# Depthwise convolution on TensorE: six channel tiles as matmuls over 4 tap groups x 32 channels

## The chip, the cores and the metric

One core of a Trainium2 chip. The time is device microseconds (us) of one execution of the whole program. A core has five engines that work beside each other, each through its own queue in order: TensorE (PE; its weight loads are listed apart as PEld), VectorE (DVE), ScalarE (ACT), GpSimd (POOL) and SyncE (SP), which here issues nearly all transfers.

## What is computed

A trunk of four layers over 256 tokens of 1024 channels. Each layer adds a token mixer and then a squared-ReLU feed-forward of width 4096. The mixers are retention, Conformer convolution, stick-breaking attention, retention. The change touches the convolution, which occurs once:

```
h = xn @ pw1_w + pw1_b
a, gate = jnp.split(h, 2, axis=-1)
h = a * jax.nn.sigmoid(gate)
h = lax.conv_general_dilated(            # depthwise: each channel by itself,
    h, dw_w[:, None, :].astype(h.dtype), # 31 taps, causal
    window_strides=(1,), padding=[(CONV_WIDTH - 1, 0)],
    dimension_numbers=('NWC', 'WIO', 'NWC'), feature_group_count=D_MODEL) + dw_b
h = layer_norm(h, ln_w, ln_b)
h = jax.nn.silu(h).astype(xn.dtype)
return h @ pw2_w + pw2_b
```

All is float32.

## The kernel before

Activations lie with channels on partitions: eight channel tiles of 128 partitions x 256 tokens. Weights stream from memory once, in a fixed order, on SP's queue: `unit` (L324) loads a chunk of 1 MB into one of three buffers `raw`; a chunk holds two units of 128x1024, and each unit is split into a high part `wh` by ACT (L336) and a low part `wl` by DVE (L337), in a pool of five. A buffer `raw` is loaded again when DVE has split its second unit.

The convolution starts with the first pointwise projection, pair of tiles by pair (`pair_b`, matmuls L456 to L458 into PSUM tiles `acc`); for each pair DVE and ACT compute the gated unit (`gate_in` L874, L877; `glu` L882, L887) and leave the result behind 30 zero columns in a tile `hc`. So tap w of a tile is the slice of 256 columns from w on.

The 31 taps of the eight tiles are shared out by hand:
- tile 0 on DVE (`tap_dve`, L927: multiply and add into PSUM tiles `mis`), later tiles 6 and 7 (into `acc`) and part of tile 5;
- tile 1, then tile 4 and the rest of tile 5 on ACT and POOL (`tap_pool`: ACT multiplies, L934, POOL adds, L936);
- tiles 2 and 3 and six taps of tile 5 on PE (`tap_pe`, L939): a diagonal 128x128 stationary matrix, built by POOL (L864) long before, times the slice of 256 columns, in fp32; each such matmul is two records in the trace.

The layer norm needs sums over all channels. `shift_a` takes column sums of finished tile 1 (L373), `shift_b` copies them (DVE, L967) and broadcasts them by two matmuls (L380) and an ACT copy (L384); the result `Gb` is subtracted from every tile when it is finished: `fin` (L980, L981), `fin_pe` (L984, one DVE instruction that reads PSUM), `fin_5` (L990 to L993). `stats` squares the tile on ACT (L945) and adds column sums of values and squares, four matmuls with one moving column for each tile (L373). The sums go to DVE (`lnv`, L1042), then mean, rsqrt, two broadcasts (L380), `warm` (L281: matmuls on ones that nothing reads), normalisation (POOL L1053, DVE L1061, ACT L1062), the split into high and low parts (L348, L349) and the second projection `out_proj`.

The order inside the stage is a table: each step is given a place on an axis by the numbers in `TP`, the steps are sorted by it (`ev`, `at`), and PE, DVE, POOL and ACT each keep that program order (`manual_schedule`). Weight chunks are issued and split where the program's own order and the buffers let them.

Of the kernel before, what the change touches and what calls it, by code (L numbers as in the profile page):

```python
# [8 lines left out]
F32 = mybir.dt.float32  # L9
# [6 lines left out]
P = 128  # L16
# [13 lines left out]
DST = 6  # chunk with which the first decay table comes  # L30
# order of the steps in stick-breaking attention
# [6 lines left out]
# order of the steps in the convolution: each group's place on one axis  # L38
TP = dict(
    pe2=42, pe3=0.0, pe5=4.4, po1=5.8, po1s=0.5, dv0=15.2, dv0s=1.05, po4=40.0, dv6=52.4,  # L40
    po5=64.8, dv5=80.5, sum1=38.7, sha=43.5, shb=44.0, shc=52.5, st1=55.1, fi0=50.0, st0=56.4,
    fi2=64.2, st2=71, fi4=71.4, st4=75.6, fi6=77.81, fi3=80.43, st6=80.2, st3=86.12, fi5=84.2,
    st5=95.3,
)
# taps of channel tile 5 on PE and on DVE
PE5, DV5 = 6, 7
# [72 lines left out]
# ---------------------------------------------------------------- parameter columns  # L119
def _param_cols():  # L120
    off, cols = 0, {}

    def add(key, n):
        nonlocal off
        cols[key] = off
        off += n

    add("norm_mix", DEPTH * 8)
    add("norm_ffn", DEPTH * 8)
    add("final", 8)  # L130
# [6 lines left out]
    add("dww", 8 * CW)  # L137
# [14 lines left out]
def _pack_params(inp):  # L152
# [16 lines left out]
    for t in range(8):  # L169
        out[:, PCOL["dww"] + t * CW : PCOL["dww"] + (t + 1) * CW] = dw[:, t * P : (t + 1) * P].T  # L170
# [26 lines left out]
def _consts():  # L197
# [10 lines left out]
    put("o32", np.full((P, 32), 1 / DK))  # L208
    put("sel", (r[:, None] // 32 == np.arange(4)[None, :]) / 32)
# [21 lines left out]
class Trunk:  # L231
    def __init__(self, ctx, tc, xT, w, prm, cst, out):
# [11 lines left out]
        self.prp = pool("prp", 3)  # L244
        self.acc_p = pool("acc", 4, space=bass.MemoryType.PSUM)
# [8 lines left out]
        self.rawt = self.raw.tile([P, UPC * 1024], F32, name="raw0", tag="raw")  # L254
# [12 lines left out]
        self.raw1 = self.raw.tile([P, UPC * 1024], F32, name="raw1", tag="raw")  # L267
# [8 lines left out]
    # keeps the tensor engine's clock up where it has to wait  # L276
# [7 lines left out]
    # ---- small helpers  # L284
# [29 lines left out]
    def unit(self, key):  # L314
# [29 lines left out]
    # a k-tile to [hi | lo]  # L344
# [7 lines left out]
    # ---- rsqrt of a column tile by Newton steps  # L352
    def rsqrt(self, m, n, tag):
# [6 lines left out]
        # of third order, with a = -m y^2: y (15 + 10 a + 3 a^2) / 8 = 3/8 y ((a + 10/3) a + 5); 3/8 is left out here  # L360
# [4 lines left out]
        # Newton's step, with 3/8 taken in  # L365
# [5 lines left out]
    # column sums over partitions: dst[tok, 0] (+)= sum_p src[p, tok] * scale  # L371
# [3 lines left out]
    # [tok, 2 columns] -> [128, 256] on all partitions  # L375
# [14 lines left out]
    # ---- RMSNorm: z = x * w as hi/lo, squares summed for r  # L390
# [50 lines left out]
    # ---- weights stationary: one unit (4 k-tiles x 256 columns) into a bank [2 m-tiles x 256 tok]  # L441
# [18 lines left out]
    # the same into half a bank for each m-tile  # L460
# [13 lines left out]
    # into a bank for each m-tile: [wh zh + wl zh | wh zl]  # L474
# [43 lines left out]
    # ---- feed-forward  # L518
# [42 lines left out]
    # ---- final RMSNorm: x * w turned to rows, scaled per token on the way out  # L561
# [28 lines left out]
    # x * w to rows, two pairs to a bank for each token tile  # L590
# [9 lines left out]
    # the last pair, its second m-tile after its first  # L600
# [50 lines left out]
    # ---- retention  # L651
    def retention(self, j, nxt):
# [34 lines left out]
        # mean squares: each head on 32 rows beside the others, then per token [tok, (token tile, q or k, head)]  # L687
# [8 lines left out]
        # per-token factors  # L696
# [19 lines left out]
        for h in range(RH):  # L716
# [5 lines left out]
            for t in range(2):  # L722
# [8 lines left out]
                else:  # L731
                    # token tile 0, seen by all tokens, as hi and lo
# [100 lines left out]
    # ---- activations stationary: one unit (2 k-tiles x 512 columns) into two banks [tok, 512]  # L833
# [13 lines left out]
    # ---- Conformer convolution  # L847
    def conv(self, j, nxt):
# [4 lines left out]
        todo = [(2, w) for w in range(CW)] + [(3, w) for w in range(CW)] + [(5, w) for w in range(CW - PE5, CW)]  # L853
        dgs = {}

        # diagonal stationary operands, four taps to a tile
        for i in range(0, len(todo), 4):
            d = self.bigt()
            grp = todo[i : i + 4]
            while grp:  # L860
                t, w = grp[0]
                n = sum(1 for x in grp if x[0] == t)
                o = (4 - len(grp)) * P if len(todo[i : i + 4]) == 4 else (len(todo[i : i + 4]) - len(grp)) * P
                nc.gpsimd.tensor_mul(  # L864
                    v3(d[:, o : o + n * P], n, P), self.id.unsqueeze(1).to_broadcast([P, n, P]),
                    self.p("dww", t * CW + w, n).unsqueeze(2).to_broadcast([P, n, P]),
                )
                for e in range(n):
                    dgs[t, w + e] = d[:, o + e * P : o + (e + 1) * P]
                grp = grp[n:]  # L870
# [9 lines left out]
        def glu(p, pa, sg):  # L880
            va = self.tmp()
            nc.vector.tensor_mul(v3(va, 2, S), v3(pa, 2, S), self.b2(rb))  # L882
            for f in range(2):
                s = slice(f * S, (f + 1) * S)
                o = self.bigt()
                nc.gpsimd.memset(o[:, : CW - 1], 0.0)
                nc.vector.scalar_tensor_tensor(  # L887
                    out=o[:, CW - 1 : CW - 1 + S], in0=va[:, s], scalar=self.p("pw1b", 2 * p + f), in1=sg[:, s],
# [19 lines left out]
        tap = lambda t, w: hc[t][:, w : w + S]  # L908
        wc = lambda t, w: self.p("dww", t * CW + w)
# [4 lines left out]
        r0, r1, r4, r5 = halves(self.mis), halves(self.bigt), halves(self.bigt), halves(self.bigt)  # L914
        r6, r7, pb2, pb3 = self.acc()[:, :S], self.acc()[:, :S], self.acc(), self.acc()
        pb2, pb3, pb5 = pb2[:, :S], pb3[:, :S], pb2[:, S:]

        # running sums of taps; the first op of a sum starts it
# [350 lines left out]
```

## Time and profile before

| | |
|---|---|
| three runs | 1398.76, 1400.78, 1402.77 us; median 1400.78 |
| the profiled execution, its span | 1399.4 us (no other time of it is listed) |
| PE, DVE, ACT, POOL busy | 99%, 73%, 57%, 14% of the span |
| first pointwise projection of the convolution | 404 to 446 us |
| taps, shift and column sums | 446 to 492 us |
| norm, then the second projection from 499 us on | 492 to 524 us |

In the tables that follow, a row of a timeline gives start, duration, engine, source line, operation, names written and read, shapes, how many instructions follow each other, and in brackets the idle time just before with the instruction that ended it. Busy times of PE overlap, since matmuls are pipelined; the distance between starts tells what one costs.

### The profile page before, as it was taken

Reading aid. Unit: us, or ns where it says so; the run is one execution under the profiler, and the core shown is the slowest. Engines: PE = TensorE matmul, PEld = TensorE weight load, DVE = VectorE, ACT = ScalarE, POOL = GpSimd, SP = SyncE. Lnnn points to the kernel's source line nnn. Section 1 sums busy time; section 2 is a strip of 40 time slices with the busy share of each in tenths; the row PEclk is TensorE's granted clock in tenths of the full one; section 3 lists DMA queues with packets and bytes.
Section 4 is the critical chain, followed back from the end, with each engine's and each line's share of the span. In section 5 each row is a group of like instructions: output and inputs, shape, how many; then the busy total and the mean of one; then the engine's idle time right before and its main releaser. Section 6 shows DMA issues by size and latency. Waiting matters only on the chain.

```text
span 1399.4 us, 22116 instructions
## 1 busy us (share of the span) xinstructions
PE 1378.7 (99%) x8742; PEld 1239.7 (89%) x8742; DVE 1015.0 (73%) x1725; ACT 798.0 (57%) x1213; POOL 194.2 (14%) x189
## 2 busy tenths in 40 slices
PE   8999999999998999999999999999999999999998
PEld 6789999888998888888988898888987999988887
DVE  6976778775679978765578578765587687788643
ACT  6645456664457656655468666654565455555442
POOL 3201003000259920000000010000110010100011
PEclk9999999999999999999999999999999999999999
DMA  7554445555554025555543345555454444555550
GB/s 266 199 181 146 156 151 208 184 181 190 174 181 169 10 91 187 202 183 183 195 179 136 114 158 185 200 187 184 178 181 153 171 140 170 181 181 183 192 192 35
DMA packets 34808, 235.77 MB, mean 168 GB/s; under 512 B 3984, under 2 KB 4624, under 8 KB 7056
## 3 DMA queue, kind: packets, MB, share of 16 engines
q1 hardware_dynamic: 34416, 233.83, 47.1%
q8 instruction: 68, 1.11, 0.3%
q10 hardware_dynamic: 288, 0.52, 0.1%
q14 instruction: 36, 0.29, 0.1%
HBM read 233.29 MB, written 1.05 MB: 167 GB/s over the span
## 4 chain that ended last, share of the span: by engine, by line
PE 94%; DVE 3%; issue 1%; ACT 1%; DMA 1%; SPq 0%; DVEq 0%; ACTq 0%
PE acc L483 32%; PE acc L484 17%; PE acc L458 8%; PE acc L457 8%; PE acc L456 8%; PE acc L843 4%; PE acc L844 4%; PE acc L845 4%; PE acc L939 2%; PE mis L373 1%; DVE wl L337 1%; DVE mis L927 1%; PE mis L380 1%; PE acc L472 1%; PE acc L471 1%
## 5 line engine op out<-in xcount | busy, mean ns | idle before, releaser
L337 DVE TENSOR_TENSOR wl<-raw,wh 128x1024 fp32r<-128x1024 f32 (+1 forms) x442 | 555.1, 1257 | 290.5 <-ACT wh L336 285.5
L336 ACT CAST wh<-raw 128x1024 fp32r<-128x1024 f32 (+1 forms) x442 | 461.6, 1045 | 426.8 <-PE acc L483 213.9
L483 PE MATMUL acc<-z,wh 128*128 128x512 f32 x1248 | 438.1, 396 | 6.1 <-ACT wh L336 3.3
L484 PE MATMUL acc<-z,wl 128*128 128x256 f32 x1248 | 348.4, 282 | 0.2 <-DVE wl L337 0.2
L483 PEld LDWEIGHTS acc<-z,wh 128*128 128x128 f32 x1248 | 233.4, 188 | 62.3 <-ACT wh L336 4.4
L483 PE MATMUL acc<-big,wh 128*128 128x512 f32 x768 | 267.7, 393 | 0.0
L484 PEld LDWEIGHTS acc<-z,wl 128*128 128x128 f32 x1248 | 236.2, 189 | 3.0 <-DVE wl L337 1.5
L484 PE MATMUL acc<-big,wl 128*128 128x256 f32 x768 | 215.2, 280 | 0.0
L483 PEld LDWEIGHTS acc<-big,wh 128*128 128x128 f32 x768 | 143.8, 187 | 32.7
L457 PE MATMUL acc<-big,wh 128*128 128x256 f32 x576 | 162.3, 283 | 1.0 <-DVE big L349 1.0
L456 PE MATMUL acc<-big,wh 128*128 128x256 f32 x576 | 161.4, 284 | 1.1 <-DVE big L348 1.1
L458 PE MATMUL acc<-big,wl 128*128 128x256 f32 x576 | 162.3, 283 | 0.0
L484 PEld LDWEIGHTS acc<-big,wl 128*128 128x128 f32 x768 | 145.1, 189 | 0.0
L419 POOL TENSOR_TENSOR t<-t,t 128x512 f32<-128x512 f32 x25 | 39.1, 1563 | 733.7 <-DVE z L404 456.9
L456 PE MATMUL acc<-z,wh 128*128 128x256 f32 x416 | 118.3, 285 | 0.0
L458 PE MATMUL acc<-z,wl 128*128 128x256 f32 x416 | 118.1, 284 | 0.0
L457 PE MATMUL acc<-z,wh 128*128 128x256 f32 x416 | 117.8, 284 | 0.0
L457 PEld LDWEIGHTS acc<-big,wh 128*128 128x128 f32 x576 | 110.4, 192 | 1.2 <-DVE big L349 1.2
L456 PEld LDWEIGHTS acc<-big,wh 128*128 128x128 f32 x576 | 109.5, 192 | 2.1 <-DVE big L348 1.6
L458 PEld LDWEIGHTS acc<-big,wl 128*128 128x128 f32 x576 | 110.4, 192 | 0.0
L502 ACT COPY t<-acc 128x256 f32<-128x256 f32 x180 | 65.1, 371 | 58.2 <-PE acc L484 58.2
L843 PE MATMUL acc<-wh,z 128*128 128x512 f32 x224 | 87.8, 394 | 0.0
(240 smaller groups left out, 1943.6 us busy)
## 6 DMA issues: line engine op xcount, KB each, us to landing
raw<-in_w SPq DMA_DIRECT2D x216, 1024.0 KB, 4.8
raw<-in_w SPq DMA_DIRECT2D x6, 512.0 KB, 7.7
x<-in_x SPq DMA_DIRECT2D x4, 256.0 KB, 5.8
raw<-in_w SPq DMA_DIRECT2D x4, 256.0 KB, 7.4
cst<-in_cst SPq DMA_DIRECT2D x4, 192.0 KB, 5.0
cst<-in_cst SPq DMA_DIRECT2D x1, 532.0 KB, 8.8
out<-t SPq DMA_DIRECT2D x2, 256.0 KB, 2.7
out<-t ACTq DMA_DIRECT2D x2, 256.0 KB, 2.9
```

The costliest lines, as they stand in the source:

```text
L336: nc.scalar.copy(hi[:, s], src[:, s])
L337: nc.vector.tensor_sub(lo[:, s], src[:, s], hi[:, s])
L419: (nc.vector if p == 3 and self.quick else nc.gpsimd).tensor_add(a, self.sq, q)
L456: nc.tensor.matmul(o, wh[:, kk, cs], ah, start=st, stop=False, **kw)
L457: nc.tensor.matmul(o, wh[:, kk, cs], al, start=False, stop=False, **kw)
L458: nc.tensor.matmul(o, wl[:, kk, cs], ah, start=False, stop=en, **kw)
L483: nc.tensor.matmul(ps[m], wh[:, kk, cs], a, start=first and kk == 0, stop=False, **kw)
L484: nc.tensor.matmul(ps[m][:, :S], wl[:, kk, cs], a[:, :S], start=False, stop=last and kk == 3, **kw)
L502: nc.scalar.copy(o[:, s], ps[m][:, S:])
L843: nc.tensor.matmul(ps[t], zh[:, s], wh[:, kk], start=k == 0, stop=False, skip_group_check=True)
L844: nc.tensor.matmul(ps[t], zh[:, s], wl[:, kk], start=False, stop=False, skip_group_check=True)
L845: nc.tensor.matmul(ps[t], zl[:, s], wh[:, kk], start=False, stop=k == 7, skip_group_check=True)
```

## The change

Tiles 2 to 7 go to PE, tile 0 stays on DVE and tile 1 on ACT and POOL. A matmul no longer has 128 channels and one tap, but 32 channels and four taps:

- `spread(d)` writes two finished tiles `hc[d]`, `hc[d+1]` (128x287) to DRAM by two transfers and reads them back by four, each into 32 partitions: partition 32 s + c holds, for channel c of each group of 32, the row moved by 8 s columns, 263 wide. It goes into a buffer `raw`, which is 2104 columns wide instead of 2048. It is called for tiles 2, 4 and 6, on SP's queue.
- `taps_pe(d, g)`, for round g of 8: four matmuls, one for each group j of 32 channels, on the column group 32 j to 32 j + 31 of the array. The stationary operand is a strip of 128x32 with the weights of taps g - 1, g + 7, g + 15 and g + 23 (`strip`, built by POOL in 12 instructions of 128x512), the moving one 256 columns of the spread rows from column g on, the result 32 partitions of the tile's PSUM half.
- `stats(d)` is one matmul of a constant 128x32 with all 512 columns (values and squares), onto one of four column groups; ACT copies the result and four column-sum matmuls with one column finish it. The squares are steps of their own (`square`).
- Two channel tiles share one PSUM tile, `acc`.

```
+        def spread(d):
+            rows = self.dram.tile([2, 4, 32, HL], F32, name=self.nm("hd"), tag="hd")
+            for i in range(2):
+                nc.sync.dma_start(rows[i].rearrange("j c u -> (j c) u"), hc[d + i][:, :HL])
+            t = self.raw.tile([P, RAWW], F32, name=self.nm("raw"), tag="raw")
+            for s in range(4):
+                nc.sync.dma_start(
+                    v3(t[32 * s : 32 * s + 32], 8, HW),
+                    rows.rearrange("i j c u -> c (i j) u")[:, :, NG * s : NG * s + HW],
+                )
+            for i in range(2):
+                h4[d + i] = t[:, i * 4 * HW : (i + 1) * 4 * HW]
...
             pa = self.pair_b("conv_pw1_w", j, p * 256, self.zs)
+            if p == 3:
+                spread(2)
+                spread(4)
             glu(p, pa, gate_in(p, pg))
+        spread(6)
...
-        def tap_pe(t, w, o, first, last):
-            nc.tensor.matmul(o, dgs[t, w], tap(t, w), start=first, stop=last, **kw)
+        def taps_pe(d, g):
+            for j in range(4):
+                nc.tensor.matmul(
+                    pb[d][32 * j : 32 * j + 32], strip[d][g // 4][:, ((g % 4) * 4 + j) * 32 : ((g % 4) * 4 + j + 1) * 32],
+                    h4[d][:, j * HW + g : j * HW + g + S], start=g == 0, stop=g == NG - 1, **kw,
+                )
...
         def stats(d):
-            nc.scalar.activation(out=cc[d][:, S:], in_=cc[d][:, :S], func=AF.Square)
             n = L["n"]
             L["n"] += 1
-            for t in range(2):
-                for e in range(2):
-                    i = t * 2 + e
-                    self.colsum(
-                        L["st"][:, i : i + 1], cc[d][:, e * S + t * P : e * S + (t + 1) * P], self.sc(1024),
-                        n == 0 and i == 0, n == 7,
-                    )
+            o = 32 * (n % 4)
+            nc.tensor.matmul(L["st"][o : o + 32], self.c("o32", 32), cc[d], start=n < 4, stop=n > 3, **kw)
...
+        for i, d in enumerate(PET):
+            t0 = TP["pe"] + TP["pes"] * i
+            for g in range(NG):
+                at(t0 + 0.43 * g, taps_pe, d, g)
+            at(max(t0 + 3.9, TP["f2"]), fin_pe, d, pb[d])
+            at(max(t0 + 4.0, TP["f2"]), square, d)
...
+        sm, st = self.tmp(), self.mis()
+        nc.scalar.copy(sm, L["st"])
+        for t in range(2):
+            for e in range(2):
+                i = t * 2 + e
+                self.colsum(st[:, i : i + 1], sm[:, e * S + t * P : e * S + (t + 1) * P], self.sc(128))
```

Comments of the source are gone and lines have moved; the lines of the changed kernel that the order rows name are L338 and L351 (weight load and DVE's split), L883 and L886 (`spread`), L966 (`taps_pe`), L981 (`stats`), L1007 (`fin_pe`), L1043 (`lnv`).

Three places where the order of instructions matters. The first is PE at the last two channel tiles (`acc_4828` is the PSUM tile of tiles 6 and 7, `raw_4808` their spread rows, `big_4818` to `big_4821` the finished tiles 4 to 7, `mis_5026` the sums):

```order
L966 MATMUL acc_4828<-raw_4808,big_4232 32x256 x16
L981 MATMUL mis_5026<-big_4818,cst 32x512 [waits Activation_49]
L981 MATMUL mis_5026<-big_4819,cst 32x512 [waits Activation_49]
L966 MATMUL acc_4828<-raw_4808,big_4234 32x256 x4
L966 MATMUL acc_4828<-raw_4808,big_4234 32x256 [waits DVE_49]
L966 MATMUL acc_4828<-raw_4808,big_4234 32x256 x11
L966 MATMUL acc_4828<-raw_4808,big_4236 32x256 x16
L981 MATMUL mis_5026<-big_4820,cst 32x512 [waits Activation_49]
L981 MATMUL mis_5026<-big_4821,cst 32x512 [waits Activation_49]
```

Where PE ran single taps of tiles 3 and 5 in one row, it now runs the first round of tile 7 (four matmuls) and then waits for DVE, which has to read tile 6 out of the same PSUM tile. Tile 5 has the same wait for tile 4.

The second is DVE over the same time (`acc_4827` is the PSUM tile of tiles 4 and 5; `raw_5300`, `raw_5358` and `raw_5416` are the next three weight chunks):

```order
L1007 SCALAR_TENSOR_TENSOR big_4818<-acc_4827,prm,Gb_5024 128x256 [waits PE_49]
L351 TENSOR_TENSOR wl_5303<-raw_5300,wh_5302 128x1024 [waits DMAHW3_49,Activation_49]
L351 TENSOR_TENSOR wl_5331<-raw_5300,wh_5330 128x1024 [waits Activation_49]
L1007 SCALAR_TENSOR_TENSOR big_4819<-acc_4827,prm,Gb_5024 128x256 [waits PE_49]
L351 TENSOR_TENSOR wl_5361<-raw_5358,wh_5360 128x1024 [waits DMAHW4_49,Activation_49]
L351 TENSOR_TENSOR wl_5389<-raw_5358,wh_5388 128x1024 [waits Activation_49]
L1007 SCALAR_TENSOR_TENSOR big_4820<-acc_4828,prm,Gb_5024 128x256 [waits PE_49]
L351 TENSOR_TENSOR wl_5419<-raw_5416,wh_5418 128x1024 [waits DMAHW5_49,Activation_49]
L1007 SCALAR_TENSOR_TENSOR big_4821<-acc_4828,prm,Gb_5024 128x256 [waits PE_49]
L1043 COPY lnv_5188<-mis_5182 128x4 [waits PE_49]
```

Before, five splits of the second projection's weights stood among the last pointwise steps and the taps of tile 0; now four stand between the fin of tile 4 and that of tile 6.

The third is SP's queue from the spread of tiles 6 and 7 on:

```order
L883 DMA hd_4805<-big_4799 128x287 [waits DMAHW5_49,DVE_49,Pool_49]
L883 DMA hd_4805<-big_4802 128x287 [waits DMAHW6_49,DVE_49,Pool_49]
L886 DMA raw_4808<-hd_4805 32x8x263 [waits DMAHW6_49,DMAHW5_49,Activation_49]
L886 DMA raw_4808<-hd_4805 32x8x263
L886 DMA raw_4808<-hd_4805 32x8x263 [waits DMAHW1_49]
L886 DMA raw_4808<-hd_4805 32x8x263 [waits DMAHW2_49]
L338 DMA raw_5300<-in_w 128x2048 [waits DMAHW3_49,PE_49]
L338 DMA raw_5358<-in_w 128x2048 [waits DMAHW4_49,DMAHW3_49,DVE_49]
L338 DMA raw_5416<-in_w 128x2048 [waits PE_49]
L338 DMA raw_5496<-in_w 128x2048 [waits DMAHW4_49,DVE_49]
```

Before, the chunk in the first of these places followed the last chunk of the first projection at once and waited for DVE alone. Now `raw_5300` stands behind the three spreads and waits for PE, which reads the spread rows of tile 3 in that buffer; `raw_5358` goes into the buffer of `raw_5300` and waits for its landing and its split; `raw_5416` waits for the taps of tile 5.

## Rows read from the trace of the kernel before

**Rows 1.** The page: busy time of each engine, share of the span and instructions; and the chain of work that ended last, by line, as shares of the span.
```profile
PE 1378.7 (99%) x8742; PEld 1239.7 (89%) x8742; DVE 1015.0 (73%) x1725; ACT 798.0 (57%) x1213; POOL 194.2 (14%) x189
PE acc L483 32%; PE acc L484 17%; PE acc L458 8%; PE acc L457 8%; PE acc L456 8%; PE acc L843 4%; PE acc L844 4%; PE acc L845 4%; PE acc L939 2%; PE mis L373 1%; DVE wl L337 1%; DVE mis L927 1%; PE mis L380 1%; PE acc L472 1%; PE acc L471 1%
```

**Rows 2.** Windows by stage: the stretch, its length, busy time (and instructions) of PE, PEld, DVE, ACT and POOL, the granted clock of PE as a share of full speed, the share of DMA time, GB/s.
```profile
404.00:453.00 49.00, 44.96 (x365) 43.99 (x364) 44.98 (x69) 36.67 (x63) 33.26 (x33) 0.99 0.44 153
453.00:487.00 34.00, 33.74 (x160) 29.68 (x160) 32.36 (x78) 23.39 (x51) 32.80 (x48) 0.91 0.07 28
```

**Rows 3.** Timeline of PE from the last pointwise matmul to the norm.
```profile
445.80 0.28 PE L458 MATMUL acc<-z,wl 128*128 128x256 f32 x1
445.92 1.89 PE L939 MATMUL acc<-big,big 128*128 128x256 f32 x8
...
453.26 1.22 PE L380 MATMUL mis<-cst,lns 128*128 128x128 f32 x4 [2.96 <-DVE lns L967]
454.27 13.69 PE L939 MATMUL acc<-big,big 128*128 128x256 f32 x52
...
469.99 0.95 PE L373 MATMUL mis<-cst,big 128*128 128x1 f32 x8
470.80 12.34 PE L939 MATMUL acc<-big,big 128*128 128x256 f32 x56
```

**Rows 4.** Timeline of DVE, late pointwise steps and the first instruction of the norm.
```profile
441.18 1.77 DVE L887 SCALAR_TENSOR_TENSOR big<-t,prm,t 128x256 f32<-128x256 f32 x2
442.88 1.76 DVE L337 TENSOR_TENSOR wl<-raw,wh 128x1024 fp32r<-128x1024 f32 x1
...
449.59 0.67 DVE L882 TENSOR_TENSOR t<-acc,rb 128x512 f32<-128x512 f32 x1
450.19 1.21 DVE L337 TENSOR_TENSOR wl<-raw,wh 128x1024 fp32r<-128x1024 f32 x1
451.32 1.81 DVE L887 SCALAR_TENSOR_TENSOR big<-t,prm,t 128x256 f32<-128x256 f32 x2
...
492.13 0.16 DVE L1042 COPY lnv<-mis 128x4 f32<-128x4 f32 x1 [2.00 <-PE mis L373]
```

**Rows 5.** Groups of instructions by line, engine and shape, from 430 to 560 us (the last one from 300 to 400 us): count, busy time, mean ns of one, idle time before them.
```profile
L936 POOL TENSOR_TENSOR big<-big,pr 128x256 f32<-128x256 f32 x63 | 51.3, 854 | 2.6 <-ACT pr L934 2.6
L337 DVE TENSOR_TENSOR wl<-raw,wh 128x1024 fp32r<-128x1024 f32 x28 | 37.9, 1352 | 8.8 <-ACT wh L336 8.5
L336 ACT CAST wh<-raw 128x1024 fp32r<-128x1024 f32 x27 | 28.2, 1045 | 10.3 <-PE acc L457 6.3 <-PE acc L483 3.4 <-ACT t L414 0.5
L927 DVE SCALAR_TENSOR_TENSOR acc<-big,prm,acc 128x256 f32<-128x256 f32 x60 | 23.7, 476 | 0.0
L945 ACT ACTIVATE big<-big 128x256 f32<-128x256 f32 x8 | 3.0, 405 | 5.2 <-DVE big L993 5.0 <-POOL big L972 0.2
L984 DVE SCALAR_TENSOR_TENSOR big<-acc,prm,Gb 128x256 f32<-128x256 f32 x2 | 1.0, 477 | 1.5 <-PE acc L939 1.5
...
L864 POOL TENSOR_TENSOR big<-cst,prm 128x512 f32<-128x512 f32 x11 | 16.9, 1562 | 15.8 <-PE acc L458 15.8
```

**Rows 6.** Timeline of PE in the first retention layer, at the column sums that go to 32 rows for each head (L690; two heads at 54.92, one at 73.37) and the instruction after each.
```profile
54.92 1.05 PE L690 MATMUL mis<-big,cst 128*32 128x512 f32 x4
55.90 0.50 PE L483 MATMUL acc<-z,wh 128*128 128x512 f32 x1
...
73.37 1.04 PE L690 MATMUL mis<-big,cst 128*32 128x512 f32 x2
74.35 0.50 PE L844 MATMUL acc<-wl,z 128*128 128x512 f32 x1
```

**Rows 7.** Timeline of PE in stick-breaking attention, at matmuls onto two groups of 64 columns.
```profile
793.53 0.65 PE L1201 MATMUL mis<-big,big 128*64 128x256 f32 x4
793.96 0.44 PE L1204 MATMUL mis<-big,big 128*64 128x128 f32 x4
794.18 0.65 PE L1201 MATMUL mis<-big,big 128*64 128x256 f32 x4
```

**Rows 8.** The page's DMA issues (count, KB each, median us from issue to landing), and the timeline of SP's queue around the stage.
```profile
raw<-in_w SPq DMA_DIRECT2D x216, 1024.0 KB, 4.8
cst<-in_cst SPq DMA_DIRECT2D x4, 192.0 KB, 5.0
out<-t SPq DMA_DIRECT2D x2, 256.0 KB, 2.7
...
444.66 7.09 SPq L324 DMA_DIRECT2D raw<-in_w  x2
508.84 3.93 SPq L324 DMA_DIRECT2D raw<-in_w  x2
```

**Rows 9.** Windows of 2 us after PE's idle time before 453.26, columns as in rows 2.
```profile
454.00:456.00 2.00, 2.00 (x8) 1.64 (x7) 1.97 (x4) 1.48 (x4) 0.96 (x2) 0.50 0.77 324
456.00:458.00 2.00, 2.00 (x6) 1.64 (x5) 2.00 (x6) 1.54 (x4) 2.00 (x4) 0.50 0.00 0
458.00:460.00 2.00, 2.00 (x8) 1.64 (x8) 2.00 (x6) 1.47 (x4) 2.00 (x4) 0.77 0.00 0
460.00:462.00 2.00, 2.00 (x11) 1.73 (x11) 2.00 (x6) 1.47 (x4) 2.00 (x4) 1.00 0.00 0
```

**Rows 10.** ACT's copy of the per-head sums (L691): count, duration in ns (min, median, max), first and last start, shapes.
```profile
L691 ACT COPY t<-mis x2: 587/587/587, 74.5 to 1064.1; 128x512 f32<-128x512 f32 x2
```

More of the change, by code (lines that the diff above doesn't have):

```diff
@@ L39 @@
 TP = dict(
[L40 to L43, printed above, removed]
-)
-PE5, DV5 = 6, 7
+    po1=5.8, po1s=0.82, dv0=15.2, dv0s=0.9, sum1=40.0, sha=47.4, shb=50.9, shc=51.2, sq1=52.0, fi0=51.3,
+    pe=44.0, pes=3.5, f2=51.5, st0=57.95, st4=61.45, st6=69.5,
+)
+PET = (2, 3, 4, 5, 6, 7)
+DVT = (0, 1)
+NG = 8
+HW = S + NG - 1
+HL = S + CW
+RAWW = 8 * HW
 MANUAL = {mybir.EngineType.DVE, mybir.EngineType.PE, mybir.EngineType.Pool, mybir.EngineType.Activation}
@@ L136, in _param_cols @@
     add("pw1b", 16)
-    add("dww", 8 * CW)
+    add("dww", len(DVT) * CW)
+    add("dwp", len(PET) * NG * 4)
     add("dwb", 8)
@@ L168, in _pack_params @@
     dw = inp["conv_dw_w"][0]
-    for t in range(8):
-        out[:, PCOL["dww"] + t * CW : PCOL["dww"] + (t + 1) * CW] = dw[:, t * P : (t + 1) * P].T
+    for i, t in enumerate(DVT):
+        out[:, PCOL["dww"] + i * CW : PCOL["dww"] + (i + 1) * CW] = dw[:, t * P : (t + 1) * P].T
+    for i, t in enumerate(PET):
+        for g in range(NG):
+            for s in range(4):
+                if g + s:
+                    v = dw[g + NG * s - 1, t * P : (t + 1) * P].reshape(4, 32).T
+                    o = PCOL["dwp"] + (i * NG + g) * 4
+                    out[32 * s : 32 * s + 32, o : o + 4] = v
     put("dwb", inp["conv_dw_b"][0])
@@ L208, in _consts @@
     put("o32", np.full((P, 32), 1 / DK))
+    put("id32", np.tile(np.eye(32), (4, 1)))
     put("sel", (r[:, None] // 32 == np.arange(4)[None, :]) / 32)
@@ L266, in __init__ @@
             nc.sync.dma_start(self.rawt[:, s], w[0][:, s])
-        self.raw1 = self.raw.tile([P, UPC * 1024], F32, name="raw1", tag="raw")
+        self.raw1 = self.raw.tile([P, RAWW], F32, name="raw1", tag="raw")
         for o in range(0, UPC * 1024, 1024):
@@ L852, in conv @@
         rb = None
[L853 to L863, printed above, removed]
+        strip, h4 = {}, {}
+        for i, d in enumerate(PET):
+            strip[d] = []
+            for b in range(NG // 4):
+                o = self.bigt()
                 nc.gpsimd.tensor_mul(
-                    v3(d[:, o : o + n * P], n, P), self.id.unsqueeze(1).to_broadcast([P, n, P]),
-                    self.p("dww", t * CW + w, n).unsqueeze(2).to_broadcast([P, n, P]),
-                )
-                for e in range(n):
-                    dgs[t, w + e] = d[:, o + e * P : o + (e + 1) * P]
-                grp = grp[n:]
+                    v3(o, 16, 32), self.c("id32", 32).unsqueeze(1).to_broadcast([P, 16, 32]),
+                    self.p("dwp", (i * NG + b * 4) * 4, 16).unsqueeze(2).to_broadcast([P, 16, 32]),
+                )
+                strip[d].append(o)
+        def spread(d):
[3 more added lines that the diff above has]
+            t = self.raw.tile([P, RAWW], F32, name=self.nm("raw"), tag="raw")
+            for s in range(4):
+                nc.sync.dma_start(
[4 more added lines that the diff above has]
+                h4[d + i] = t[:, i * 4 * HW : (i + 1) * 4 * HW]
         def gate_in(p, pg):
@@ L913, in conv @@
         halves = lambda t: (t()[:, :S], t()[:, :S])
-        r0, r1, r4, r5 = halves(self.mis), halves(self.bigt), halves(self.bigt), halves(self.bigt)
-        r6, r7, pb2, pb3 = self.acc()[:, :S], self.acc()[:, :S], self.acc(), self.acc()
-        pb2, pb3, pb5 = pb2[:, :S], pb3[:, :S], pb2[:, S:]
+        r0, r1 = halves(self.mis), halves(self.bigt)
+        pb, pbs = {}, [self.acc() for _ in range(3)]
+        for i, d in enumerate(PET):
+            pb[d] = pbs[i // 2][:, (i % 2) * S : (i % 2 + 1) * S]
         def tap_dve(t, w, a, first=False, bias=False):
@@ L1020, in conv @@
         at(TP["shc"], shift_c)
-        at(TP["st1"], stats, 1)
+        at(TP["sq1"], square, 1)
         at(TP["fi0"], fin, 0, *r0)
-        at(TP["st0"], stats, 0)
-        at(TP["fi2"], fin_pe, 2, pb2)
-        at(TP["st2"], stats, 2)
-        at(TP["fi4"], fin, 4, *r4)
-        at(TP["st4"], stats, 4)
-        at(TP["fi6"], fin, 6, r6, None)
-        at(TP["fi6"] + 0.01, fin, 7, r7, None)
-        at(TP["fi3"], fin_pe, 3, pb3)
-        at(TP["st6"], stats, 6)
-        at(TP["st6"] + 0.01, stats, 7)
-        at(TP["st3"], stats, 3)
-        at(TP["fi5"], fin_5)
-        at(TP["st5"], stats, 5)
+        at(TP["fi0"] + 0.5, square, 0)
+        for t0, ds in (("st0", (0, 1, 2, 3)), ("st4", (4, 5)), ("st6", (6, 7))):
+            for i, d in enumerate(ds):
+                at(TP[t0] + 0.001 * i, stats, d)
         with self.tc.manual_schedule(engines=MANUAL):
```

50 lines of the change are left out of this document (14 added, 36 removed).

## The prediction

> **What bounds the kernel now.** The page comes first. PE is busy nearly all of the span and the chain that ended last runs through it, but the taps of this convolution (L939) hold only 2% of that chain [rows 1]: the change can move one short stage, so I left the shares at once and went to that stage. The windows by stage show it: between 404 and 453 us PE multiplies by the pointwise weights, from 453 to 487 the four arithmetic engines are nearly all full, PE with taps, DVE with taps, POOL with adds, while DMA is almost idle [rows 2]. PE's own timeline gives the two ends of what can be saved: the last pointwise matmul starts at 445.80 and the first tap at 445.92; the first instruction that reads the norm's sums, DVE's lnv copy, starts at 492.13 [rows 3, 4]. **The stage lasts 46.2 us.** Everything before it stays, everything after it (mean, rsqrt, broadcast, second projection) stays too, so the gain is 46.2 minus the new length.
>
> Why it is that long: 31 taps for each of eight channel tiles are spread over three kinds of workers. A tap costs PE two records, 0.433 us (52 records in 13.69 us, less the pipeline's tail, and 56 in 12.34) [rows 3], DVE 0.476 us, and the pair ACT and POOL 0.854 us, POOL's add being the longer [rows 5]. All finish near 486 to 490, so the work is balanced and only cheaper taps shorten it.
>
> **The change, part by part.**
>
> *Taps.* One matmul now takes four taps of 32 channels instead of one tap of 128, and four of them, on four column groups of the array, form a round. If the four run beside each other, a round costs what one old tap did, 0.433 us, and does four taps: a channel tile is 8 rounds, 3.46 us, where 31 taps took 13.4. Six tiles: 48 rounds, **20.8 us** on PE. Do column groups run beside each other? The trace has two places. With two heads on two column groups, four records start at 54.92 and the next instruction at 55.90, 0.98 us; with one head, two records start at 73.37 and the next at 74.35, also 0.98 [rows 6]. So two groups cost what one costs. And with two groups of 64 columns the stick-breaking matmuls come four records in 0.43 us for 256 columns and four in 0.22 for 128, eight in 0.65, time after time [rows 7]. Four groups at once no row shows, nor 54 ns for each record over a long stretch: 0.22/4 is 54 ns in a burst, 0.65/8 is 81 ns over both. These are the bounds of a round: 8 records at 54 ns, 0.433, at best; 8 at 81, 0.65; and two groups at a time, 0.87. I take 0.433, because the 256-column records, the nearest row, were limited by their columns (four in 0.43 with two groups in use) and not by their number. The Trainium skill ("TensorE: Matmul & The Clock Gate", Part 3, measured speedup) lists 2.38 instead of 3 for three column tiles; by that share a round would be an estimated 0.55 us and the taps 5.4 us longer; no run here shows three.
>
> *Order on PE.* Tiles 2 to 7 follow each other from 445.9 with the shift's column sums (0.47) behind tile 2, its broadcast (two matmuls, about 0.5 at full clock, 1.01 between starts at half) behind tile 3, four stats matmuls (0.98 as in rows 6) behind tile 5, two more behind tile 6. So: 445.9 + 3.46 + 0.47 + 3.46 = 453.3; + 0.5 + 3.46 = **457.3**, tile 4 done.
>
> *Waits that this adds.* Two tiles share a PSUM tile, and the order rows show the second round of tiles 5 and 7 behind DVE's fin of tiles 4 and 6. Tile 5: fin 4 takes 0.48 [rows 5], with handovers PE stands some 0.7; tile 5 ends at 461.5, stats to 462.5, tile 6 at **466.0**, stats 4 and 5 at 466.9, the first round of tile 7 at 467.4. Tile 7 then needs fin 6, and fin 6 stands on DVE behind four splits of weight chunks. The first of those chunks goes into the buffer that tile 3's spread rows leave, the second into the same buffer again, when the first has been split. A chunk of 1 MB takes 4.8 us from issue to landing [rows 8]; ACT's cast 1.05, DVE's split 1.22 where nothing slows it (1.21 at 450.19; the mean is 1.35) [rows 4, 5]. So 453.4 + 4.8 + 1.05 + 2 x 1.22 = 461.7, then again 4.8 + 1.05 + 2.44 = 470.0, fin 6 done at **470.5**: PE idles 3 us, beside 0.1 us for the handover.
>
> *Clock.* In the trace of before an idle of 2.96 us before 453.26 left the granted clock at half for some 5.6 us (0.50 from 454 to 458, 0.77 in the next two, 1.00 after) [rows 3, 9]. I let the idle here do the same: 7 rounds at 0.87 are 6.1 us, to **476.6**.
>
> *Tail.* fin 7 0.48, square 0.41 [rows 5], two stats matmuls 0.98, ACT's copy of 128x512 0.59 [rows 10], eight column-sum records 0.95 [rows 3], handovers and half clock 0.7 together: lnv copy at 480.7. **Gain 492.1 - 480.7 = 11.4 us.**
>
> *What I cost at nothing.* Strips: POOL builds 12 tiles of 128x512 where it built 19 diagonal ones, at 1.56 us each [rows 5]; the feed-forward before covers them, POOL being idle there; without that cover, 19 us. Row transfers for tiles 2 and 3, and 4 and 5: two writes and four reads on SP's queue, with the nearest rows 2.7 us for a store of 256 KB and 5.0 for a load of 192 KB [rows 8]; GLU of tiles 4 and 5 ends near 443 (441.18 + 1.77) [rows 4], so tile 4's rows land by 451 where PE wants them at 453.9. For tiles 6 and 7: DVE no longer splits the three units that it split from 442.88 to 451.4 [rows 4], so their GLU, 0.67 for L882 and 1.81 for two of L887 behind the last matmul [rows 4], ends near 448.7 and not at 453.1; plus 2.7 and 4.8, 456.2, wanted at 462.5. Without the cover each lost microsecond is one on the path. Tile 0 on DVE and tile 1 on ACT and POOL go at the same prices and end before 450, since the same splits are gone. The second projection's weights come later: before, two loads were issued from 444.66 on and none from 451.8 to 508.84 [rows 8]; now they land at 458, 466 and after, and five units are split and the next chunks landed before it starts. Nothing is added there.
>
> The sum is made against the profiled span, 1399.4 us; the median of the three runs, 1400.78 (1398.76 to 1402.77), lies 1.4 above it, which is start and end around the span or the scatter of runs. I put the gain on the median: 1400.8 - 11.4 = **1389.4 us**.
>
> **Rivals.**
>
> *B, the wait or the half clock fails to come.* At full clock the seven rounds give 3.0 back: gain 14.4 to 14.8, 1386. If fin 6 isn't late at all: gain 17.8, 1383. For it: 4.8 us is a median over loads of which many queue behind each other; one alone may land sooner. Against: two loads in series through one buffer are in the order rows.
>
> *C, PE's pace is that of the mixed row.* 0.65 us for a round: a tile 5.2 us. Then tile 3 ends at 456.8 and the splits of two chunks at 473.4, but tile 6 only at 474.6: fin 6 is no longer late, the taps end at 480.8, lnv comes 3.9 later at 484.7: gain 7.4, 1393.4. For it: 81 ns for each record is the best long stretch in the trace. Against: that stretch was bound by columns.
>
> *D, the spread rows are slow.* Reads of 1052-byte rows into 32 partitions each; four in series at 2.7 us would be 10.8 instead of 4.8. The rows of tiles 6 and 7 then land at 462, and the weight chunk behind them in SP's queue 6 us later, and with it fin 6: gain 2 to 5, 1396 to 1399. For it: no row shows such a transfer, and the queue is one. Against: DMA moves little here, 0.07 of its time [rows 2].
>
> *E, slower.* The groups go two at a time, or the two passes of a matmul are held in program order, so that each next group starts with the second pass of the one before: a round is 0.87. Forty-eight are 41.6 us; with both waits for fin at 0.5, shift and broadcast 1.0, stats 1.85 + 0.98, the taps end at 492.3, and the tail of 3.9 makes lnv 496.2, 4.1 later than before: **1404.9**. It decides from a round of some 0.78 us on. Against: the records of two groups start together [rows 6]. For: four were never seen. The Trainium skill (same page, Part 3, the mechanism) says that matmuls start and end strictly in program order; by that rule E would follow if the passes alternate. The trace's two-group row speaks against it.
>
> **How the numbers follow.** Chances: mine 0.46, B 0.14, C 0.13, D 0.12, E 0.15. A measurement of this kernel tells about 0.3%, 4.2 us, from no change: the lines are 1396.6 and 1405.0. Faster: mine, B, C and a third of D, 0.77. Same: the rest of D and a third of E, 0.13. Slower: the rest of E with whatever is added to it, 0.10. The range goes from B's lower end, 1383, to just beyond D, 1400, and leaves out E.
>
> **What would show it.** In the profile after: L966 in groups of 16 records each 0.87 us (two rounds at full clock); PE's idle of 3 us at 467 put down to DVE L1007; the granted clock at 0.50 after it; two loads some 8 us apart by SP; lnv at 480 to 481. Records starting 0.1 us apart in a round show C or E; a wait of L966 on DMA shows D; no wait in tile 7 shows B. Wrong altogether is a gain outside 1 to 18 us.

## The result, and the profile after

The changed kernel takes 1391.54 us (median of 4 runs, 1390.3 to 1392.4), the kernel before 1401.12 in the same comparison: a ratio of 0.9937, with an interval of 0.9925 to 0.9950. That is 9.6 us saved, where 11.4 were forecast. The profiled spans are 1389.5 and 1399.4 us. In the profiled runs the stage, from the first tap at 444.99 to lnv (DVE's first reading of the norm's sums) at 482.91, takes 37.9 us, where it took 46.2 and 34.8 were forecast: 8.3 us were won in it and 0.7 behind it (from lnv to the end of the span are 906.6 us, before 907.3). The other 0.9 us is a first tap that came earlier; kernels that are alike up to there differ in it by as much as 2.0 us (443.9 to 445.9). The taps went as forecast; what was given back is larger than forecast, and in the place that was named.

PE's timeline answers to [rows 3] (start, length, engine, line, operation, shapes, count, and in brackets the idle time before with what ended it):

```profile
444.99 3.67 PE L966 MATMUL acc<-raw,big 128*32 128x256 f32 x64
...
449.13 3.67 PE L966 MATMUL acc<-raw,big 128*32 128x256 f32 x64
452.73 0.71 PE L394 MATMUL mis<-cst,lns 128*128 128x128 f32 x4
...
462.01 3.65 PE L966 MATMUL acc<-raw,big 128*32 128x256 f32 x64
...
467.29 0.60 PE L966 MATMUL acc<-raw,big 128*32 128x256 f32 x2
474.30 4.74 PE L966 MATMUL acc<-raw,big 128*32 128x256 f32 x56 [6.42 <-DVE big L1007]
478.88 1.02 PE L981 MATMUL mis<-big,cst 128*32 128x512 f32 x2
...
481.82 1.05 PE L387 MATMUL mis<-cst,t 128*128 128x1 f32 x8 [0.68 <-ACT t L1036]
```

A tile of 31 taps takes 3.6 us from start to start (449.13 to 452.73), with 64 records; it took 13.4 us. Then, after the first round of tile 7, PE stands still for 6.42 us, and the seven rounds that follow take 4.58 us, not 3.0.

DVE's timeline over the same stretch, for [rows 4], shows who kept PE waiting:

```profile
457.55 0.48 DVE L1007 SCALAR_TENSOR_TENSOR big<-acc,prm,Gb 128x256 f32<-128x256 f32 x1 [2.00 <-PE acc L966]
463.15 2.36 DVE L351 TENSOR_TENSOR wl<-raw,wh 128x1024 fp32r<-128x1024 f32 x2 [5.11 <-ACT wh L350]
465.42 0.48 DVE L1007 SCALAR_TENSOR_TENSOR big<-acc,prm,Gb 128x256 f32<-128x256 f32 x1
471.49 2.36 DVE L351 TENSOR_TENSOR wl<-raw,wh 128x1024 fp32r<-128x1024 f32 x2 [5.59 <-ACT wh L350]
473.77 0.48 DVE L1007 SCALAR_TENSOR_TENSOR big<-acc,prm,Gb 128x256 f32<-128x256 f32 x1
...
482.91 0.16 DVE L1043 COPY lnv<-mis 128x4 f32<-128x4 f32 x1 [3.31 <-PE mis L387]
...
484.36 0.16 DVE L378 SCALAR_TENSOR_TENSOR vy<-vt,vy 128x2 f32<-128x2 f32 x1
484.56 0.71 DVE L380 TENSOR_TENSOR vt<-vy 128x2 f32<-128x2 f32 x1
```

DVE is idle for more than 5 us twice (5.11 and 5.59), waiting for ACT's cast of a weight chunk, and fin 6 (DVE's instruction that finishes tile 6, 473.77) stands behind the splits of both chunks. The chain of waits, traced back from the first matmul after the idle time, names what lay behind the casts (start, length, what):

```profile
453.12 8.93 DMA raw<-in_w
...
462.07 1.05 ACT wh L350
...
463.15 2.37 DVE wl L351 x2
...
465.54 4.86 DMA raw<-in_w
```

The second chunk took 4.9 us, the first 8.9. The windows (columns as in [rows 2]) show the DMA engines over that time, and the clock during and after the idle time; the page's DMA issues add the prices of the new transfers:

```profile
455.00:457.00 2.00, 2.00 (x44) 1.19 (x40) 0.55 (x2) 1.42 (x4) 0.00 (x0) 1.00 1.16 213
459.00:461.00 2.00, 2.00 (x44) 1.19 (x40) 0.00 (x0) 0.00 (x0) 0.00 (x0) 1.00 0.65 266
469.00:471.00 2.00, 0.00 (x0) 0.00 (x0) 0.00 (x0) 0.58 (x1) 0.00 (x0) 0.89 1.02 422
475.00:477.00 2.00, 2.00 (x24) 0.92 (x20) 0.38 (x1) 0.00 (x0) 0.00 (x0) 0.50 0.71 274
477.00:479.00 2.00, 2.00 (x37) 1.06 (x30) 0.00 (x0) 0.00 (x0) 0.00 (x0) 0.90 0.55 225
```

```profile
raw<-hd SPq DMA_DIRECT2D x12, 263.0 KB, 5.3
hd<-big SPq DMA_DIRECT2D x6, 143.5 KB, 3.0
```

While the spread rows are read, the DMA engines are as busy as with a weight chunk (1.16 against 1.02) and move half as much (213 against 422 GB/s).

### The profile page after: what moved, and what is told of

Same layout as the page of the kernel before. It is cut to its first block, busy times and chain, and to the rows that moved or that the text cites. A ratio compares the mean times of both kernels' runs of the same rounds, so it can differ in the third digit from the quotient of the medians.

```text
span 1389.5 us, 22352 instructions
## 1 busy us (share of the span) xinstructions
PE 1367.6 (98%) x8950; PEld 1218.2 (88%) x8950; DVE 984.6 (71%) x1656; ACT 775.2 (56%) x1165; POOL 145.7 (10%) x133
## 4 chain that ended last, share of the span: by engine, by line
PE 95%; DMA 2%; DVE 1%; ACT 1%; issue 0%; SPq 0%; DVEq 0%; ACTq 0%
PE acc L497 33%; PE acc L498 17%; PE acc L470 9%; PE acc L472 9%; PE acc L471 9%; PE acc L857 4%; PE acc L858 4%; PE acc L859 4%; DMA raw<-in_w 2%; PE acc L966 1%; PE mis L387 1%; PE acc L486 1%; PE acc L484 1%; PE acc L485 1%; PE mis L394 1%; DVE wl L351 1%
## 5 line engine op out<-in xcount | busy, mean ns | idle before, releaser
L351 DVE TENSOR_TENSOR wl<-raw,wh 128x1024 fp32r<-128x1024 f32 (+1 forms) x442 | 552.5, 1252 | 299.9 <-ACT wh L350 295.1
```

What stands on the lines that cost most here:

```text
L351: nc.vector.tensor_sub(lo[:, s], src[:, s], hi[:, s])
```

## The experiments

The theory: fin 6 is late because it stands behind the four splits of two weight chunks in DVE's queue, and the first chunk is late because the reads of the spread rows fill the DMA engines. Rivals: the shared PSUM tile, the reused buffer, SP's queue. A first table compares lengths, since the first tap comes at 443.9 to 445.9 in the different kernels; "to lnv" is the time from the first tap to the first reading of the norm's sums, and "to projection" the time from there to the first matmul of the second projection.

| kernel | first tap | to lnv | to projection | median us | ratio to before |
|---|---|---|---|---|---|
| before | 445.92 | 46.2 | 7.1 | | |
| the change | 444.99 | 37.9 | 8.0 | 1391.54 | 0.9937 (0.9925 to 0.9950) |
| e1, four PSUM tiles | 445.14 | 36.7 | 7.1 | 1389.76 | 0.9924 (0.9909 to 0.9939) |
| e2, fins first | 443.89 | 30.0 | 8.9 | 1386.57 | 0.9903 (0.9888 to 0.9918) |
| e5, reads on ACT's queue | 445.68 | 38.6 | 8.0 | 1392.36 | 0.9944 (0.9926 to 0.9962) |
| e7, splits in gaps | 444.15 | 28.7 | 8.0 | 1381.06 | 0.9870 (0.9853 to 0.9886) |
| e8, four buffers | 444.08 | 40.7 | 7.0 | 1392.43 | 0.9950 (0.9935 to 0.9965) |
| e9, clock kept up | 445.88 | 36.3 | 7.1 | 1390.40 | 0.9938 (0.9923 to 0.9953) |
| e10, POOL held | 444.58 | 28.5 | 6.6 | 1382.45 | 0.9880 (0.9864 to 0.9897) |
| e6, sums only | 444.31 | 48.1 | 7.1 | 1402.42 | 1.0021 (1.0011 to 1.0030) |

Where an expectation below counts 37.2 us for the change or 29.1 for e2, it does so from a record behind the first tap; 37.9 and 30.0 are right.

**Do column groups run beside each other?** Two kernels change only the order of the matmuls of a tile, all rounds of one group and then the next:

```
-        def taps_pe(d, g):
-            for j in range(4):
+        def taps_pe(d, g, j0):
+            for j in (j0,):
...
-            for g in range(NG):
-                at(t0 + 0.43 * g, taps_pe, d, g)
+            for q in range(4):
+                for g in range(NG):
+                    at(t0 + 0.43 * (2 * q + g / 4), taps_pe, d, g, q)
```

> The change with the matmuls of a tile in another order: all eight rounds of one column group, then those of the next. Same matmuls, same counts. Theory (a round costs what one matmul costs because four column groups run beside each other): matmuls on one group follow each other at 0.433 us, a tile takes 13.9 us instead of 3.5, six tiles 83 us; the wait for the weights is covered, lnv comes some 55 us later: 1445 us. Rival (a tile of 128x32 is cheap by its size alone, with no overlap needed): as the change, 1391 us.

and eight rounds on groups 0 and 1, then eight on 2 and 3:

> The change with the matmuls of a tile in two halves: eight rounds on column groups 0 and 1, then eight on groups 2 and 3. Theory (groups run beside each other, each matmul 0.433 us): a tile takes 6.9 us, twice that of four groups; if it goes as in turn, where 32 matmuls took 11.5 us and not 13.9, 5.8. The waits for the weights are covered: 1398 to 1404 us. Rival (PE's pace is set by the number of instructions, not by groups): 3.6 us a tile, 1391 us.

Measured in one run each: 1426.72 and 1395.76 us. PE's timelines, in turn first, then two groups, one tile per row of 64:

```profile
456.26 11.51 PE L966 MATMUL acc<-raw,big 128*32 128x256 f32 x64
467.70 0.71 PE L394 MATMUL mis<-cst,lns 128*128 128x128 f32 x4
```

```profile
451.08 6.28 PE L966 MATMUL acc<-raw,big 128*32 128x256 f32 x64
457.29 0.71 PE L394 MATMUL mis<-cst,lns 128*128 128x128 f32 x4
```

The same 32 matmuls take 11.4, 6.2 and 3.6 us with one, two and four groups in alternation. So the groups do run beside each other, and the count of instructions is not what sets the pace. In turn I expected 13.9 us (32 times 0.433) and got 2.4 us less. Two narrower windows of that run, the first inside the row of one group, the second where it ends and the next one's begins, show why:

```profile
444.52 2.54 PE L966 MATMUL acc<-raw,big 128*32 128x256 f32 x11
446.68 1.27 PE L966 MATMUL acc<-raw,big 128*32 128x256 f32 x9
```

Inside the row, ten records start in 2.16 us, so a matmul alone on one group takes 0.43 us, as much as a round of four in the change. Where the group changes, nine records take 1.27 us instead of eleven in 2.54: the last matmuls of one group run beside the first of the next. That is why both runs came out below what I expected, and why the 11.4 us are not the price of one group alone: by that price, 13.9, four groups gain nearly fourfold.

**Is sharing a PSUM tile the cause?** e1 gives tiles 4 and 5 a PSUM tile each, and lets 6 and 7 use the halves beside 2 and 3:

```
-        pb, pbs = {}, [self.acc() for _ in range(3)]
+        pb, pbs = {}, [self.acc() for _ in range(4)]
         for i, d in enumerate(PET):
-            pb[d] = pbs[i // 2][:, (i % 2) * S : (i % 2 + 1) * S]
+            pb[d] = pbs[i % 4][:, (i // 4) * S : (i // 4 + 1) * S]
```

> The change as it is, with one edit: the PSUM halves are shared out over four tiles, 2 with 6, 3 with 7, 4 alone and 5 alone, so that no round on PE waits for a fin. Theory (the wait of 6.4 us in tile 7 comes from the two weight chunks that DVE splits ahead of fin 6, and PE is only where it shows): PE runs through tile 7 and ends its taps near 470.4, but fin 6 still comes at 473.8 and fin 7 behind one more split at 475.9, so lnv comes at 479.3 to 480.5 instead of 482.9: 1388 to 1389 us. Rival (sharing a PSUM tile is the cause): the 6.4 us of idle and the 1.5 us of half clock go, lnv near 475: 1383 us.

```profile
467.94 4.04 PE L966 MATMUL acc<-raw,big 128*32 128x256 f32 x58
475.82 1.04 PE L981 MATMUL mis<-big,cst 128*32 128x512 f32 x2 [3.84 <-ACT big L975]
477.34 1.92 PE L981 MATMUL mis<-big,cst 128*32 128x512 f32 x2 [0.48 <-ACT big L975]
```

PE ran through tile 7 and then waited in the column sums for the square of tile 6, whose fin came at 474.84. The wait moved by one step (3.84 us in its new place, 1.2 us less in all up to lnv); the sums that followed ran at half clock (1.92 instead of 1.04), which I had priced too low. The rival falls.

**Is the buffer the cause, or the queue order?** e8 has four buffers: `pool("raw", 4)`, and `pool("big", 32)` to make room.

> The change with four buffers of the size of a chunk instead of three (and 32 instead of 36 activation tiles, to make room). The first weight chunk then waits for no tap and the second doesn't wait for the first one's split, but the program puts two splits ahead of fin 4 and five ahead of fin 6 on DVE. Theory (a fin behind splits in DVE's queue is the cause, whatever buffer they use): the wait moves from tile 7 to tile 5, where fin 4 comes at 464 to 465 instead of 457.6, and a smaller one stays at tile 7: 1389 to 1392 us. Rival (the reused buffer is the cause): both waits go: 1383 us.

```profile
465.37 6.08 PE L966 MATMUL acc<-raw,big 128*32 128x256 f32 x56 [8.81 <-DVE big L1007]
...
477.67 3.24 PE L966 MATMUL acc<-raw,big 128*32 128x256 f32 x56 [0.62 <-DVE big L1007]
```

The wait moved to tile 5, since two splits now stood ahead of fin 4, and grew to 8.8 us. No gain: without the reused buffer a fin still waits behind splits. e2 leaves the PSUM tiles and the number of buffers as they are and fixes the order: `ahead` casts and splits the next weight unit at its place in the table, two units behind fin 6, one behind fin 7, and a fourth with its cast behind ACT's copy of the sums and its split behind the rsqrt. (The second chunk then also goes into another buffer.)

```
+        for t in (62.05, 62.05, 65.6):
+            at(t, self.ahead)
...
+            nc.scalar.copy(sm, L["st"])
+            lo = self.ahead(True)
...
+            rs = self.rsqrt(m, 2, "v")
+            lo()
```

> The change with another order on DVE and ACT: the splits of the first two weight units stand behind fin 6, that of the third behind fin 7, that of the fourth behind the norm's rsqrt; PSUM halves shared as in the change. Theory (queue order on DVE is the cause): the wait before the second round of tile 7 vanishes, the clock stays full, the taps end near 469.9, lnv comes at 473.6 instead of 482.9: gain 9.3, 1382 us. Rival 1 (the second projection then waits for its weights): lnv as said, but the first matmul of the second projection some 4 us later than 8 us behind lnv: 1386 us. Rival 2 (the spread rows of tiles 6 and 7 or PSUM sharing hold tile 7): a wait of more than 2 us stays: 1388 us or more.

```profile
466.45 3.24 PE L985 MATMUL acc<-raw,big 128*32 128x256 f32 x56 [0.63 <-DVE big L1026]
...
482.79 0.97 PE L489 MATMUL acc<-big,wh 128*128 128x256 f32 x4 [3.40 <-DVE big L381]
```

DVE's timeline of e2, the two splits behind fin 6, lnv, and two more splits behind it:

```profile
467.81 2.36 DVE L366 TENSOR_TENSOR wl<-raw,wh 128x1024 fp32r<-128x1024 f32 x2 [1.42 <-ACT wh L365]
...
473.88 0.16 DVE L1066 COPY lnv<-mis 128x4 f32<-128x4 f32 x1 [0.67 <-PE mis L406]
...
476.54 1.21 DVE L366 TENSOR_TENSOR wl<-raw,wh 128x1024 fp32r<-128x1024 f32 x1
477.67 1.74 DVE L371 TENSOR_TENSOR wl<-raw,wh 128x1024 fp32r<-128x1024 f32 x1
```

The wait at tile 7 fell from 6.42 to 0.63 us and lnv came 30.0 us behind the first tap instead of 37.9, as the theory says. But not all of these 7.9 us arrived: two splits now stood in the norm, between the rsqrt and the normalisation, the projection started 8.9 us behind lnv after an idle of 3.4, and its first matmuls ran at half clock (0.50 from 484 to 488). From lnv to the end of the span e2 takes 911.0 us, the change 906.6, so 3.5 us are left in the profiled runs; the medians differ by 5.0. That is rival 1 in kind, with splits in place of late weights.

**Why was the first chunk late?** e5 issues the four reads for tiles 6 and 7 on ACT's queue: `(nc.scalar if d == 6 else nc.sync).dma_start(...)`.

> The change with the four reads of tiles 6 and 7 issued on ACT's queue instead of SP's. Theory (the first weight chunk took 8.9 us instead of 4.8 because it stood in the same queue behind these reads): the chunk, issued near 453 as now, lands at 459 to 460 instead of 462, the reads a little later but before 462; fin 6 comes 2 to 2.5 us earlier: 1389 us. Rival (the 16 DMA engines are full with both, whatever the queue): the chunk lands at 461 to 462 as now: 1391 to 1392 us.

The chain of waits of e5, from the first chunk to its cast:

```profile
453.55 10.09 DMA raw<-in_w
...
463.66 1.05 ACT wh L350
```

The chunk took 10.1 us on a queue of its own. My theory of the queue falls; the DMA engines themselves are full with the short rows, as the windows above show. The two kernels with another order of matmuls confirm it: there tile 3 ends later, and its buffer comes free when the reads are over. The first chunk in the chain of waits of e11:

```profile
457.40 4.81 DMA raw<-in_w
```

The DMA share between 456 and 458 is 0.16 there, and the chunk takes 4.8 us. In e4 it is issued at 467.80 and its cast starts at 472.64, 4.8 us again. So in these runs the first chunk is late where it meets the reads, and only there.

**What did the half clock cost?** e9 puts 28 matmuls on ones into the idle time: `at(TP["pe"] + 5 * TP["pes"] + 0.2, self.warm, 28)`.

> The change with 28 matmuls on ones, which nothing reads, on PE between the first and the second round of tile 7, 6 us at full clock, inside its idle time of 6.4 us. Theory (the idle left the granted clock at half and cost tile 7 some 1.5 us: 4.6 us for seven rounds instead of 3.0): the clock stays at 1.00 and lnv comes 1.5 us earlier: 1390 us. Rival (idle time and clock are not linked): lnv at the same place, 1391.5 us.

```profile
468.59 6.22 PE L295 MATMUL mis<-ones 128*128 128x512 bf16 x27
475.01 3.25 PE L966 MATMUL acc<-raw,big 128*32 128x256 f32 x56 [0.21 <-DVE big L1007]
478.09 1.02 PE L981 MATMUL mis<-big,cst 128*32 128x512 f32 x2
```

Seven rounds took 3.08 us instead of 4.58. The stage was 1.7 us shorter (36.25 instead of 37.92), 1.5 of it in these rounds, and the median 1.1 us less, though the two ratios don't separate: the timelines show the mechanism and its size, the runs' times don't resolve it.

**The new column sums alone.** e6 is the kernel before with the new `stats` and the copy and sums behind it.

> The kernel before with one part of the change, the column sums: one matmul of 128x32 by 512 columns for each tile, then ACT's copy and four column sums. Theory (the old sums were hidden but for the last tile's, and the new ones add a copy and a second step behind the last tile): lnv comes 1.5 to 3 us later than before: 1402 to 1403.5 us. Rival (the 40 records that ended the stage, 5.6 us, were on the path): several us earlier, 1396 us.

It came out 3.0 us slower by the medians; in the profiled runs the stage is 1.8 us longer. In e6 the last part of tile 5 is ready earlier, but the norm isn't:

```profile
487.81 0.42 DVE L988 TENSOR_TENSOR big<-big,big 128x256 f32<-128x256 f32 x1
492.36 0.16 DVE L1042 COPY lnv<-mis 128x4 f32<-128x4 f32 x1 [4.13 <-PE mis L373]
```

From the last tile's result to lnv are 4.1 us; before it was 2.0 [rows 4]. The sums alone are a loss; no run shows whether the old ones would cost more in the changed kernel's shorter stage.

**Everything in the gaps.** e7 has e1's PSUM tiles and the splits where DVE and ACT have nothing to do: `for t in (60.0, 60.0, 62.05, 62.05, 65.6): at(t, self.ahead)`, that is two behind fin 5, two behind fin 6, one behind fin 7.

> Both edits together, and the splits moved into DVE's and ACT's idle time: PSUM halves over four tiles; the splits of the first two weight units behind fin 5, of the next two behind fin 6, of the fifth behind fin 7, none between the column sums and the normalisation. Theory (queue order on DVE is the cause, and what the order of fins ahead of splits gave back went to the splits that stood in the norm): PE runs through all taps, lnv comes 27.9 us after the first tap (37.2 in the change, 29.1 with fins ahead of splits), the first matmul of the second projection 8 us after it as in the change: 1382 us. Rival 1 (the first chunk lands after 461 and fin 6 waits again): 1385 us. Rival 2 (the second projection is held by weights, or by POOL and DVE slowing each other in the norm): 9 us and more from lnv to the first matmul and a half clock behind it: 1384 to 1386 us.

```profile
460.35 3.64 PE L978 MATMUL acc<-raw,big 128*32 128x256 f32 x64
463.82 0.60 PE L993 MATMUL mis<-big,cst 128*32 128x512 f32 x2
...
470.01 1.04 PE L993 MATMUL mis<-big,cst 128*32 128x512 f32 x2 [1.25 <-ACT big L987]
```

```profile
472.82 0.16 DVE L1057 COPY lnv<-mis 128x4 f32<-128x4 f32 x1 [0.67 <-PE mis L399]
```

No wait is left in the taps, and from the first tap at 444.15 to lnv are 28.7 us, 17.5 less than before. 1381.06 us, 18.4 us below before in the same comparison, is what the change was worth without the wait (17.8 in the prediction's rival B).

**The norm's lost microsecond.** From lnv to the projection the change takes 1.0 us more than before, and DVE's last small steps of the rsqrt take 0.65 to 0.71 us instead of 0.16 (484.56 above); POOL's subtractions of the mean start at 484.53, while before, and in e1 and e8, they start only when the last of these steps has begun, and all steps take 0.16. e10 adds to e7 a copy on POOL that reads the rsqrt ahead of POOL's subtractions: `nc.gpsimd.tensor_copy(hold, rs)`.

> The version with the splits in the gaps, and POOL's subtraction of the mean held back by a copy of two columns on POOL that reads the result of the rsqrt. Theory (while POOL subtracts, DVE's three last small steps of the rsqrt take 0.65 to 0.72 us instead of 0.16, 1.5 us in a row on the path): they take 0.16 again, the broadcast of the rsqrt starts 1.5 us earlier behind lnv, POOL some 0.6 later, the second projection 1 to 1.5 us earlier: 1380 us. Rival (the slow steps have another cause, such as writes of weights that arrive): they stay, 1381 to 1382 us.

```profile
475.09 0.16 DVE L394 SCALAR_TENSOR_TENSOR vy<-vt,vy 128x2 f32<-128x2 f32 x1
...
480.40 0.94 DVE L375 TENSOR_TENSOR big<-t,big 128x256 fp32r<-128x256 f32 x1
```

The mechanism was right: all steps took 0.16, and the projection began 6.6 instead of 8.0 us behind lnv. The time wasn't: now POOL's subtractions met DVE's normalisation (0.94 instead of 0.41), PE waited 1.6 and 1.0 us at the start of the projection and then ran at half clock (0.50 from 482 to 484), and 1382.45 us is no better than e7. The Trainium skill ("GPSIMD Engine Reference", 1. Specifications) says that POOL shares its memory interfaces with VectorE, with contention where DVE reads two operands from that memory or runs in a two-port mode. The traces agree for two operands, with 0.65 to 0.71 us beside POOL's subtractions and 0.16 without them; no run here tells which mode an instruction runs in.

## Why the prediction was right, and where it was off

- **Taps.** A round of 0.433 us and a tile of 3.46: measured 3.6 and 3.47 (462.01 to 465.48). Counted from the first tap, tile 6 was forecast done after 20.1 us (466.0) and was after 20.5 (465.48). Rivals C and E are out. Of the two rows from which the 0.433 was read, only the 56 records in 12.34 us give it; the 52 in 13.69 ran in part at half clock [rows 9]. The Trainium skill ("TensorE: Matmul & The Clock Gate", Part 3, measured speedup), with its 2.38 for three column tiles, would have made a round an estimated 0.55. The traces differ from that: a round of four takes 3.47 / 8 = 0.43 us, a matmul alone on one group 2.16 / 5 = 0.43, so nothing is lost with four; no run here has three.
- **The wait of tile 7.** Place and mechanism as forecast, size not: 6.4 us instead of 3.0. The term that was mis-sized is "a chunk of 1 MB takes 4.8 us", used twice; the second chunk took 4.9, the first 8.9, since the reads for tiles 6 and 7 were still on the DMA engines (4.8 where they were done, in e4 and e11). I had put that mechanism into rival D and left it out of my own sum, taking low DMA use before as evidence against it; but the change itself brings the traffic.
- **The clock.** Half clock after the idle came, but it cost 1.5 us and not 3.0: the clock was back some 3 us after PE resumed (0.90 between 477 and 479), where [rows 9] had shown 5.6. The two errors partly cancel: the second round of tile 7 began 4.7 us later behind the first tap than forecast, and 1.5 came back in its rounds.
- **The tail.** 4.1 us forecast, 4.0 measured (478.88 to 482.91). lnv came 37.9 us behind the first tap instead of 34.8 (482.91 instead of 480.7). The stage missed its forecast by 3.1 us, the saving of the medians by 1.8. That the total came closer is luck: 0.7 us behind lnv and 0.9 ahead of the first tap, in the profiled runs, were not in the forecast.
- **Costed at nothing.** Strips, the spread rows of tiles 2 to 5 and the later weights cost nothing: no tap waits for a transfer, and the second projection runs without its 1 us stall of before. The norm behind lnv, which I had said stays, lost 1.0 us to POOL up to the projection, and the projection gave back more (906.6 us from lnv to the end instead of 907.3).
- The prediction went to the place of the wait because the order rows put fin 6 behind four splits; e2 and e7 show that this order is the reason; e1, e8 and e5 show that PSUM tile, buffer and SP's queue are not.

## What to carry to other kernels

When a stage gets shorter, look in the queue orders for long instructions that wait for a transfer and stand ahead of a short one that the bound engine needs: they are harmless as long as the stage outlasts the transfer (in e4, with 11.4 us for a tile, five splits stand ahead of fin 6, and PE waits 0.58 us for it, at 504.78). Price a transfer together with the traffic that the change itself adds, and look where the released time lands: e2 gained 7.9 us at lnv and had 3.5 of it left at the end of its span. Here the order of five splits, with a PSUM tile more, was worth as much again as the change had brought by itself (a stage of 28.7 us instead of 37.9, and 37.9 instead of 46.2).

## What I had not expected of the hardware

- Four column groups of 32, in fp32, reach 3.6 us for 64 records over several tiles, 56 ns for each: a round of four takes what one matmul takes alone, 0.43 us. And matmuls overlap even where only neighbours in the queue differ in group (11.4 us for 13.9 of matmuls in turn).
- Reads in rows of 1052 bytes filled the DMA engines (share 1.16) at 213 GB/s, where chunks with long rows moved 422 at 1.02. The Trainium skill ("DMA: Bandwidth & Descriptors", Specifications) puts the size from which a transfer runs at line rate at 512 bytes; these rows are twice that and moved half.
